# The expert stage of a decoder block, with TensorE's work written out in a fixed order that is one expert pair out of step

## The chip, the cores and the metric

The kernel runs on one core of one Trainium2 chip. The metric is device time in microseconds (us) for one launch. TensorE (PE in the rows) does the matmuls and the transposes, VectorE (DVE) and ScalarE (ACT) take results out of PSUM, GpSimd (POOL) gathers rows through an indirect DMA, and SyncE (SP) issues the plain loads and stores.

## The reference, cut to what matters

A block of 512 tokens with 1024 features goes through a token mixer, then through a mixture of 32 experts, of which each token uses two, then through a normalisation. The change is in the experts alone:

```
def hierarchical_moe(h, w_rg, b_rg, w_re, b_re, w1, w3, w2):
    t = h.reshape(B * S, D)                      # 512 x 1024
    ...                                          # group top-1, expert top-2 -> comb (512 x 32)
    for e in range(N_EXPERTS):                   # 32
        hid = jax.nn.silu(t @ w1[e]) * (t @ w3[e])          # 1024 x 512 each
        y = y + comb[:, e:e + 1] * (hid @ w2[e]).astype(jnp.float32)   # 512 x 1024
```

All weights are float32: w1, w3 and w2 of one expert are 2 MiB each, 192 MiB for the 32 experts.

## The kernel before

Experts are taken in 16 pairs (expert p and expert p + 16). A pair has 128 slots, 64 for each of its experts, and two pairs make a group, so there are 8 groups. For a group, `fetch` marks on VectorE which token sits in which slot (`sel0`), has TensorE turn that into row numbers and weights (`slot_weights`, bank `pw`), and gathers the tokens' rows into `xg` by two indirect DMAs. `experts` then does, for the group:

- rows: 16 transposes of `xg` in four blocks into the banks `gx`; ScalarE and VectorE each scale half of a block into `xt`.
- `slot_rows`: four transposes of `sel0` per pair (bank `pbk`), copied by ScalarE to `back`, which later puts the slots' results back on their tokens.
- `layer(q, "a")` and `layer(q, "b")`: the products of pair q with w1 (`ha`) and w3 (`hb`). Each is 16 float32 matmuls of 512 columns; they alternate between the two experts of the pair, which lie in the two halves of the array's columns (`tile_position`). The profile shows each such matmul as two instructions, so a product has 32 rows.
- `turned(q)`: four transposes (bank `pht`) of the gated hidden layer, copied by ScalarE to `ht`.
- `outputs(q, ht)`: the second layer, again 32 rows, into two banks `po`; VectorE weighs them (`high`) and splits them into two parts (`ohl`), with a ScalarE copy in between.
- `combine`: eight joins per group, four matmuls each (bank `pc`), which VectorE adds to `hx`. Before, the joins of a group are put in a list, `pending`, and are written out in the next group's `turned(0)`.

The weights come in loads of 1 MiB, issued by SyncE in a fixed order, into a ring of 16 such places (18 the first time round). A load waits until the load that had its place before has been used. 13 loads are issued ahead of the expert stage; `weights(p)` issues the rest as the program goes along. Before, the order of loads is pair by pair: w1, w3, w2. The last two pairs have a special order and w2 in narrower parts (`TAIL`).

What orders the engines: SyncE is always in the order of the code. For TensorE, VectorE and ScalarE a scheduler places the instructions of the groups, by its own estimate of times, and only the end of the last group (`ORDER`) is written out by hand.

Of the kernel before, what the change touches and what calls it, by code (L numbers as in the profile page):

```python
# [8 lines left out]
F32 = mybir.dt.float32  # L9
# [16 lines left out]
H = 4  # L26
# [34 lines left out]
def kernel(ctx: ExitStack, tc: tile.TileContext, a, dbg=None):  # L61
# [17 lines left out]
    def after(ins, other):  # L79
        tc.add_manual_dep(raw_ins(ins), raw_ins(other).name, NOSYNC, reason="order")  # L80
# [659 lines left out]
    def big(tag, name, shape, dt=F32):  # L740
        return pr.tile(list(shape), dt, tag=tag, bufs=SLOTS[tag], name=name)
# [451 lines left out]
    def count_passes(last):  # L1193
        pcn = bank("g", "pcn")
        for t in range(NT):
            after(T.matmul(pcn[:, 0:NE], onesb, ohs[:, t, :], start=(t == 0), stop=(t == NT - 1)), last)
# [16 lines left out]
    WORK = {"back": 3, "wsl": 4, "h": 1}  # L1213
# [12 lines left out]

    pending = []
# [58 lines left out]
    def fetch(n, cols, name):  # L1286

        xg = cp.tile([P, 2, D], F32, tag="U", bufs=2, name="xg" + name)
        wcol = {}
        for q in range(n):  # L1290
            for t in range(NT):
                V.tensor_scalar(sel0[:, t, q * P:(q + 1) * P], slotno, cols(q)[0][:, t], None, op0=ALU.is_equal)
            wcol[q], at = slot_weights(q, cols(q), name, True)
            G.indirect_dma_start(xg[:, q], None, rowsd, bass.IndirectOffsetOnAxis(at.bitcast(U32), 0), bounds_check=S - 1, oob_is_err=False)
        return xg, wcol

    def experts(n, cols, wts, name, ready=None, following=None, early=False, tail=False, alone=False):


        NSL = n * P  # L1300
        sel2 = sel0
        if alone:
            ready = fetch(n, cols, name)
        xt = big("rows", "xt" + name, [P, ND, 2 * P])
        for kk in range(ND // 2):
            if early:
                o = gathered[kk]
            else:
                o = bank("bg" if kk % 2 == 0 else "tr", f"gx{name}{kk}")
                for k2 in range(2):  # L1310
                    for q in range(n):
                        c = k2 * 256 + q * P
                        T.transpose(o[:, c:c + P], ready[0][:, q, (2 * kk + k2) * P:(2 * kk + k2 + 1) * P], ident)
            for k2 in range(2):
                k = 2 * kk + k2
                os = o[:, k2 * 256:k2 * 256 + NSL]
                if k2 == 0:
                    last = A.activation(xt[:, k, 0:NSL], os, AF.Identity, bias=b2x[:, k:k + 1], scale=a2x[:, k:k + 1])
                else:
                    V.tensor_scalar(xt[:, k, 0:NSL], os, a2x[:, k:k + 1], b2x[:, k:k + 1], op0=ALU.mult, op1=ALU.add)  # L1320
        if early:
            for t in range(NT):
                token_weights(t, last)
        wcol = {} if early else ready[1]
        back, res = [], []

        def slot_rows(q, last_h=None):
            pt = bank("tr", f"pbk{name}{q}")
            for t in range(NT):
                tr = T.transpose(pt[:, t * P:(t + 1) * P], sel2[:, t, q * P:(q + 1) * P].bitcast(F32), ident)  # L1330
                if early:
                    after(tr, last_h)
# [6 lines left out]
        if not early:  # L1339
            slot_rows(0)  # L1340
        s1s, lasts = {}, {}
        halves = [slice(0, 2), slice(2, 4)] if tail else [slice(0, 4)]

        def layer(q, m):
# [3 lines left out]
            for k in range(ND):  # L1348
                for e in range(2):
                    ins = T.matmul(o[64 * e:64 * e + 64, :], xt[:, k, q * P + 64 * e:q * P + 64 * e + 64], w[wn, e, k // 4][:, k % 4, :],  # L1350
                                   start=(k == 0), stop=(k == ND - 1), tile_position=(0, 64 * e))
                    if early and q == 0 and m == "b" and k + e == 0:
                        after(ins, lasts["a"])
            lasts[m] = ins
# [8 lines left out]
        def turned(q):  # L1363

            if early and q == 0:
                for i in range(n):
                    slot_rows(i, lasts["b"])
                count_passes(lasts["b"])

            while pending:  # L1370
                pending.pop(0)()
            if q == 0 and n > 1 and not early:
                slot_rows(1)
# [3 lines left out]
            ht = wk("back" if tail and q == 0 else "h", f"ht{name}{q}", [P, 4, P])  # L1377
            for h in halves:
                A.copy(ht[:, h], pt.rearrange("p (f s) -> p f s", f=4)[:, h])  # L1379
            return ht  # L1380

        def hidden(q):
            layer(q, "a")
            layer(q, "b")
            return turned(q)

        def outputs(q, ht):

            w, ws = wts(q), wcol[q]
# [19 lines left out]

        def combine(qs, c0, c1, t):  # L1410
# [8 lines left out]
        if not tail:  # L1419
            pieces = [(0, 512), (512, D)]  # L1420
            for q in range(n):
                if q == n - 1 and following is not None:
                    following()
                steps = outputs(q, hidden(q))
                for c, p in enumerate(pieces):
                    for f in steps:
                        f(c, *p)
            joins = [lambda p=p, t=t: combine(range(n), *p, t) for p in pieces for t in range(NT)]
            if alone:
                for f in joins:  # L1430
                    f()
            else:
                pending.extend(joins)
            return
        m = [outputs(0, hidden(0))]
        norm, add, root, write = final(f"f{name}", layer(1, "a"))

        def second():
            layer(1, "b")
            m.append(outputs(1, turned(1)))  # L1440

        sums = {"A": (0, 512), "B": (512, 768), "C": (768, D)}

        def join(x, t):
            combine([1], *sums[x], t)
            norm(t, "ABC".index(x), *sums[x], V if (x, t) in (('A', 3), ('C', 1), ('C', 3)) else G)

        STEPS = {"M": lambda q, c: m[q][0](c, *TAIL[q][c]), "H": lambda q, c: m[q][1](c, *TAIL[q][c]), "L": lambda q, c: m[q][2](c, *TAIL[q][c]),
                 "X": second, "J": lambda c, t: combine([0], 512 * c, 512 * c + 512, t), "S": lambda t: add(t), "R": lambda t: root(t, 2), "W": lambda t: write(t, (640, 640, 640, 640)[t])}
        STEPS.update({x: lambda t, x=x: join(x, t) for x in sums})  # L1450
        ORDER = """M00 H00 L00 M01 H01 L01 M02 H02 J00 J01 L02 J02 J03 M03 H03 L03 J10 J11 J12 J13 X
                   M10 H10 L10 M11 H11 L11 M12 H12 M13 L12 H13 A0 A1 L13 M14 H14 A2 A3 L14 M15 H15
                   B0 B1 L15 B2 B3 S1 C0 R0 C1 R1 W0 C2 R2 W1 C3 R3 W2 W3"""
        with tc.manual_schedule(engines={mybir.EngineType.PE, mybir.EngineType.DVE, mybir.EngineType.Activation}):
            for step in ORDER.split():
                STEPS[step[0]](*map(int, step[1:]))

    fetched = {}
    pair_columns = lambda g: (lambda q: (sp[:, :, 2 * g + q:2 * g + q + 1], wp[:, :, 2 * g + q]))
    for g in range(NP // 2):  # L1460
        more_pairs = g + 1 < NP // 2
        experts(2, pair_columns(g), lambda q: weights(2 * g + q), f"g{g}_", fetched.get(g),
                (lambda: fetched.__setitem__(g + 1, fetch(2, pair_columns(g + 1), f"g{g + 1}_"))) if more_pairs else None, g == 0, not more_pairs)
# [3 lines left out]
    with tc.For_i(0, more):  # L1467
        V.tensor_scalar(base, base, float(CAP), None, op0=ALU.add)
        slots("m")
        with tc.For_i(0, NP) as p:  # L1470
# [7 lines left out]
            experts(1, lambda q: (spc, wpc[:, :, 0]), lambda q: got, "m_", alone=True)  # L1478
# [29 lines left out]
```

## Time and profile before

| what | value |
|---|---|
| median of 3 runs | 1057.96 us (1057.88 to 1058.51) |
| the profiled execution, its device time | 1057.19 us |
| the profiled execution, its span | 1055.5 us |
| mean granted TensorE clock over the span | 0.979 |
| TensorE busy | 982.8 us, 93% |
| VectorE, ScalarE, GpSimd busy | 55%, 32%, 18% |
| DMA | 283.96 MB, mean 269 GB/s |

The rows come from the profiled execution, so sums are made against its span of 1055.5 us; its device time is 1.7 us more, and the median of the three runs is 0.8 us above that. The expert stage begins at 531 us. A busy TensorE is not one at its peak: a matmul counts as busy from its start to its modelled end, also when its other half of the columns stands empty.

### The profile page before, as it was taken

To read this page: it belongs to the slowest core of one execution; us is meant where nothing else is said; L and a number is where in the kernel's file an instruction comes from. 1 tells how busy PE (TensorE), PEld (TensorE's weight loads), DVE (VectorE), ACT (ScalarE), POOL (GpSimd) and SP (SyncE) were. 2 spreads that over 40 slices of the span, in tenths; PEclk is the share of its full clock that TensorE was granted. 3 is DMA by queue.
4 is the path that set the end of the run, shared out by engine and by line. 5 is a ranking of instruction groups with operands and counts; after the bars stand their busy time and mean duration, and the time that the engine had idled before them with its cause. 6 is when DMAs were issued, how large, how long until landed. Compare 5 with 4: busy or idle time off the path is not lost. (4 is left out here: it accounts for less than half of the span.)

```text
span 1055.5 us, 13713 instructions
## 1 busy us (share of the span) xinstructions
PE 982.8 (93%) x5250; PEld 628.2 (60%) x5250; DVE 576.3 (55%) x1057; ACT 336.7 (32%) x685; POOL 188.8 (18%) x122
## 2 busy tenths in 40 slices
PE   7899999889898999899999999999999999999993
PEld 3678899888776888787743534443444434434342
DVE  7978998997898875953632314131141312313136
ACT  6556333346355444434931101010110101101024
POOL 4514334124322122210310000000000000000005
PEclk9999999989998999999999999999999999999997
DMA  9943233226766573589199999999999989899912
GB/s 281 239 132 81 80 96 86 61 60 191 248 222 217 149 231 99 181 305 377 61 403 421 421 421 421 420 421 418 421 409 409 422 341 414 350 408 397 332 31 82
DMA packets 122409, 283.96 MB, mean 269 GB/s; under 512 B 10819, under 2 KB 87339, under 8 KB 99044
## 3 DMA queue, kind: packets, MB, share of 16 engines
q1 hardware_dynamic: 112700, 252.21, 64.0%
q10 hardware_dynamic: 7624, 27.27, 7.6%
q0 software_dynamic: 2016, 3.56, 0.9%
q8 instruction: 43, 0.70, 0.3%
q14 instruction: 26, 0.21, 0.1%
HBM read 282.61 MB, written 4.19 MB: 272 GB/s over the span
## 5 line engine op out<-in xcount | busy, mean ns | idle before, releaser
L383 POOL TENSOR_TENSOR low<-raww,hiw 128x1024 fp32r<-128x1024 f32 x36 | 91.6, 2544 | 213.2 <-ACT hiw L409 199.6
L1398 PE MATMUL pog<-p_w,htg 128*64 128x512 f32 x448 | 121.1, 599 | 7.0 <-ACT htg L1379 7.0
L392 PE MATMUL fmw<-uhi,low 128*128 128x512 f32 x224 | 91.3, 408 | 0.0
L392 PE MATMUL fmw<-ulo,hiw 128*128 128x512 f32 x224 | 90.5, 404 | 0.0
L69 DVE SCALAR_TENSOR_TENSOR conv<-z,cols,conv 128x511 f32<-128x511 f32 (+14 forms) x120 | 88.6, 738 | 3.5
L392 PE MATMUL fmw<-uhi,hiw 128*128 128x512 f32 x224 | 89.8, 401 | 0.0
L1398 PEld LDWEIGHTS pog<-p_w,htg 128*64 128x64 f32 x448 | 38.5, 136 | 69.8 <-issue 59.1
L66 DVE TENSOR_TENSOR s1g<-s1g,hbg 128x512 f32<-128x512 f32 (+1 forms) x18 | 11.1, 627 | 124.9 <-PE hbg L1350 114.3
L1415 PE MATMUL pcg<-ohlg,backg 128*128 128x512 f32 (+1 forms) x264 | 71.7, 407 | 5.4 <-DVE hx L66 2.4
L69 DVE SCALAR_TENSOR_TENSOR pog<-pog,wslg,ga2r 128x512 f32<-128x512 f32 (+2 forms) x38 | 25.6, 674 | 93.1 <-PE pog L1398 92.2
L66 DVE TENSOR_TENSOR hx<-hx,pcg 128x512 f32<-128x512 f32 (+1 forms) x76 | 49.0, 655 | 46.9 <-PE pcg L1415 46.6
L392 PE MATMUL tm<-hiw,ulo 128*128 128x256 f32 x256 | 74.0, 290 | 0.0
L392 PE MATMUL tm<-low,uhi 128*128 128x256 f32 x256 | 73.8, 289 | 0.0
L392 PE MATMUL tm<-hiw,uhi 128*128 128x256 f32 x256 | 73.6, 289 | 0.0
L409 ACT CAST hiw<-raww 128x1024 fp32r<-128x1024 f32 x44 | 46.0, 1047 | 81.6 <-issue 43.4
L1415 PEld LDWEIGHTS pcg<-ohlg,backg 128*128 128x128 f32 x264 | 46.6, 190 | 37.2 <-issue 9.0
L1403 ACT CAST ohlg<-pog 128x512 fp32r<-128x512 f32 (+2 forms) x38 | 19.6, 517 | 109.9 <-DVE pog L69 95.4
L392 PEld LDWEIGHTS tm<-hiw,uhi 128*128 128x128 f32 x256 | 49.7, 195 | 0.8 <-issue 0.5
L392 PEld LDWEIGHTS tm<-low,uhi 128*128 128x128 f32 x256 | 49.7, 194 | 0.7 <-issue 0.2
L392 PEld LDWEIGHTS tm<-hiw,ulo 128*128 128x128 f32 x256 | 49.8, 194 | 0.5 <-issue 0.2
L1379 ACT COPY htg<-phtg 128x512 f32<-128x512 f32 (+1 forms) x18 | 9.5, 538 | 124.0 <-PE phtg L1376 115.8
L392 PEld LDWEIGHTS fmw<-uhi,low 128*128 128x128 f32 x224 | 42.7, 190 | 9.7
(454 smaller groups left out, 1923.7 us busy)
## 6 DMA issues: line engine op xcount, KB each, us to landing
p_w<-in_w SPq DMA_DIRECT2D x182, 1024.0 KB, 14.9
raww<-in_w_in SPq DMA_DIRECT2D x44, 512.0 KB, 4.0
adaw<-in_w_ada SPq DMA_DIRECT2D x32, 256.0 KB, 5.7
aw_ga<-in_w_ada ACTq DMA_DIRECT2D x8, 1024.0 KB
p_w2part<-in_w SPq DMA_DIRECT2D x12, 512.0 KB, 10.4
aw_a<-in_w_ada ACTq DMA_DIRECT2D x4, 1024.0 KB
aw_b<-in_w_ada ACTq DMA_DIRECT2D x4, 1024.0 KB, 7.3
aw_bf<-in_w_ada_f ACTq DMA_DIRECT2D x4, 1024.0 KB, 5.9
```

The costliest lines, as they stand in the source:

```text
L66: return V.tensor_tensor(out, in0, in1, op=op)
L69: return V.scalar_tensor_tensor(out, in0, scalar, in1, op0=op0, op1=op1)
L383: (V if turn[0] % LO_EVERY < lo_v[0] else G).tensor_tensor(lo, raw, hi.bitcast(F32), op=ALU.subtract)
L392: ins = T.matmul(*args, **kw)
L409: copy = A.copy(hi, raw)
L1379: A.copy(ht[:, h], pt.rearrange("p (f s) -> p f s", f=4)[:, h])
L1398: T.matmul(o[64 * e:64 * e + 64, :], ht[:, f, 64 * e:64 * e + 64], w["w2", e, c][:, f, :] if tail else w["w2", e, f // 2][:, f % 2, c0:c1] ...
L1403: A.copy(ohl[:, 0, c0:c1], prods[c])
L1415: T.matmul(o, back[z][:, t * P:(t + 1) * P], res[z][:, i, c0:c1], start=(z == qs[0] and i == 0), stop=(z == qs[-1] and i == 1))
```

## The change

TensorE's order in the expert stage is now written out by hand for all groups, and one pair is put between a pair's products and its second layer: w1 of a pair, then the transposes of the pair before, then w3, then the second layer of the pair before. The loads follow that order of use: w1 and w3 of pair p, then w2 of pair p - 1. `back` moves into the unused half of the tile that `xg` has, so that the buffers of the hidden layer can be three. VectorE and ScalarE are still placed by the scheduler.

```diff
-    order2 = [(0, 0, 8), (1, 0, 4), (0, 8, 12), (1, 4, 13)]
-    todo = [step for steps in todo[:-2] for step in steps] + [step for i, b, e in order2 for step in todo[NP - 2 + i][b:e]]
+    order2 = [(1, 0, 4), (0, 8, 12), (1, 4, 13)]
+
+    use = list(todo[0][0:8])
+    for p in range(1, NP - 1):
+        use += todo[p][0:8] + todo[p - 1][8:12]
+    todo = use + [step for i, b, e in order2 for step in todo[NP - 2 + i][b:e]]
...
-        while todo and count[0] < 12 * p + len(order):
+        while todo and count[0] < 12 * p + 8 + len(order):
...
-    WORK = {"back": 3, "wsl": 4, "h": 1}
+    WORK = {"back": 1, "wsl": 4, "h": 3}
...
-        xg = cp.tile([P, 2, D], F32, tag="U", bufs=2, name="xg" + name)
+        both = cp.tile([P, 4, D], F32, tag="U", bufs=2, name="xg" + name)
+        xg, room = both[:, 0:2], both[:, 2:4]
...
-            b = wk("back", f"back{name}{q}", [P, S], F32R)
+            b = rooms[0][:, 0, q * S:(q + 1) * S].bitcast(F32R)
...
+    with tc.manual_schedule(engines={mybir.EngineType.PE}):
+        for g, x in enumerate(X):
+            before = X[g - 1] if g else None
+            x["rows"](fetched)
+            if g:
+                x["slot_rows"](0)
+                x["slot_rows"](1)
+            x["layer"](0, "a")
+            if g:
+                before["turned"](1)
+            x["layer"](0, "b")
+            if g:
+                before["second"](1)
             else:
-                pending.extend(joins)
...
+                x["slot_rows"](0)
+                x["slot_rows"](1)
+                count_passes()
+            if g < NGR - 1:
+                fetched = fetch(2, pair_columns(g + 1), f"g{g + 1}_")
+            silu = x["layer"](1, "a")
+            x["turned"](0)
+            if g:
+                before["joins"]()
+            if g < NGR - 1:
+                x["layer"](1, "b")
+                x["second"](0)
+            else:
+                x["ending"](silu)
```

`second(q)` is the second layer of a pair, `joins()` the eight joins of a group, and `ending` the tail of the last group, in the same hand-written `ORDER` as before.

Where a group begins, this is what stood on TensorE before (the pair that ends is `pog_1`, the group that begins has `hag_0` and `xtg__6875`; the eight joins are `pcg`):

```order
L1398 MATMUL pog_10_6851<-p_w_6790,htg_1_6848 64x512
L1398 MATMUL pog_11_6863<-p_w_6790,htg_1_6848 64x512
L1330 MATMUL pbkg_1_7020<-ident,sel_4372 128x128 x4
L1398 MATMUL pog_10_6851<-p_w_6792,htg_1_6848 64x512
...
L1415 MATMUL pcg_000_6972<-ohlg_1_6850,backg_1_6717 128x512
L1350 MATMUL hag_0_6935<-p_w_6794,xtg__6875 64x512
L1415 MATMUL pcg_000_6972<-ohlg_1_6850,backg_1_6717 128x512
L1415 MATMUL pcg_100_6978<-ohlg_0_6726,backg_0_6601 128x512 x2
...
L1415 MATMUL pcg_05120_6996<-ohlg_0_6726,backg_0_6601 128x512
L1350 MATMUL hag_0_6935<-p_w_6796,xtg__6875 64x512
L1350 MATMUL hag_0_6935<-p_w_6794,xtg__6875 64x512
```

The scheduler had cut the products into pieces of one, two or seven matmuls and put transposes and joins between them. In the changed kernel the same place, where a group begins, reads:

```order
L1380 MATMUL pog_01_6532<-p_w_6287,htg_0_6451 64x512
L1380 MATMUL pog_01_6532<-p_w_6289,htg_0_6451 64x512
L1318 MATMUL gxg_0_6545<-ident,xgg__6372 128x128 x4
L1318 MATMUL gxg_1_6552<-ident,xgg__6372 128x128 x4
L1318 MATMUL gxg_2_6559<-ident,xgg__6372 128x128 x4
L1318 MATMUL gxg_3_6566<-ident,xgg__6372 128x128 x4
L1337 MATMUL pbkg_0_6573<-ident,sel_4372 128x128 x4
L1337 MATMUL pbkg_1_6579<-ident,sel_4372 128x128 x4
L1350 MATMUL hag_0_6609<-p_w_6291,xtg__6544 64x512
L1350 MATMUL hag_0_6609<-p_w_6293,xtg__6544 64x512
...
L1364 MATMUL phtg_1_6628<-ident,s1g_1_6444 128x128 x4
```

Here the six blocks of transposes stand together, with no product among them, and the 16 matmuls of each product follow each other, the two experts in turn.

On VectorE in the changed kernel, at the same place, the weighing of the second layer (`pog`), its split (`ohlg`) and the scaling of the rows (`xtg`) stand in this order:

```order
L69 SCALAR_TENSOR_TENSOR pog_01_6532<-pog_01_6532,wslg_0_6076,ga2r 128x512
L66 TENSOR_TENSOR ohlg_0_6519<-pog_01_6532,ohlg_0_6519 128x512
L1325 TENSOR_SCALAR xtg__6544<-gxg_0_6545,a2x,b2x 128x256
L1325 TENSOR_SCALAR xtg__6544<-gxg_1_6552,a2x,b2x 128x256
L1325 TENSOR_SCALAR xtg__6544<-gxg_2_6559,a2x,b2x 128x256
L1295 TENSOR_SCALAR sel_4372<-slotno,sp 128x128 x4
L1325 TENSOR_SCALAR xtg__6544<-gxg_3_6566,a2x,b2x 128x256
```

In the kernel before, the scaling of a group's rows stood ahead of the weighing of the pair that ended:

```order
L1320 TENSOR_SCALAR xtg__6567<-gxg_2_6582,a2x,b2x 128x256
L1292 TENSOR_SCALAR sel_4372<-slotno,sp 128x128 x4
L69 SCALAR_TENSOR_TENSOR pog_10_6543<-pog_10_6543,wslg_1_6160,ga2r 128x512
L69 SCALAR_TENSOR_TENSOR pog_11_6555<-pog_11_6555,wslg_1_6160,ga2r 128x512
L66 TENSOR_TENSOR ohlg_1_6542<-pog_10_6543,ohlg_1_6542 128x512
```

So the rows' scaling moved behind the last weighing and split of the pair before.

## Rows read from the trace of the kernel before

**Rows 1.** Windows: stretch, its length, busy us by engine, TensorE clock, DMA share, GB/s.
```profile
540.00:560.00 20.00, 20.00 (x112) 8.67 (x110) 4.85 (x21) 1.76 (x3) 2.21 (x2) 1.00 1.02 421
...
760.00:780.00 20.00, 18.98 (x82) 8.81 (x79) 9.01 (x20) 3.68 (x7) 0.00 (x0) 1.00 1.01 420
780.00:800.00 20.00, 18.44 (x83) 7.73 (x83) 3.88 (x9) 1.74 (x3) 1.98 (x2) 1.00 0.99 394
...
900.00:920.00 20.00, 19.99 (x76) 8.70 (x72) 8.30 (x13) 1.76 (x3) 0.00 (x0) 1.00 0.86 345
```

**Rows 2.** Timeline, TensorE (start, length): second transposes of the third and seventh groups.
```profile
688.81 0.66 PE L1376 MATMUL phtg<-ident,s1g 128*128 128x128 f32 x4 [0.84 <-DVE s1g L66]
...
953.10 0.66 PE L1376 MATMUL phtg<-ident,s1g 128*128 128x128 f32 x4 [0.58 <-DVE s1g L66]
```

**Rows 3.** Timeline of TensorE, a product cut into pieces.
```profile
903.45 1.07 PE L1350 MATMUL hag<-p_w,xtg__6875 128*64 128x512 f32 x2
...
908.00 3.65 PE L1350 MATMUL hag<-p_w,xtg__6875 128*64 128x512 f32 x14
```

**Rows 4.** Waits of TensorE from 530 us: us in total, times, longest.
```profile
PE phtg L1376 <- DVE s1g L66: 9.8, 14, 0.9
PE pog L1398 <- ACT htg L1379: 7.5, 12, 0.7
```

**Rows 5.** Timeline of TensorE, products and joins that stand in one piece.
```profile
594.87 3.06 PE L1415 MATMUL pcg<-ohlg,backg 128*128 128x512 f32 x12
597.77 0.60 PE L1330 MATMUL pbkg<-ident,sel 128*128 128x128 f32 x4
...
938.30 7.09 PE L1350 MATMUL hag<-p_w,xtg__6875 128*64 128x512 f32 x32
945.17 7.09 PE L1350 MATMUL hbg<-p_w,xtg__6875 128*64 128x512 f32 x32
```

**Rows 6.** Timeline, the rows of the fourth group and who takes them out.
```profile
696.23 1.53 PE L1313 MATMUL gxg<-ident,xgg__5827 128*128 128x128 f32 x12
697.14 1.48 ACT L1318 ACTIVATE xtg__5951<-gxg,b2x,a2x 128x256 f32<-128x256 f32 x3 [7.05 <-PE gxg L1313]
697.74 1.46 DVE L1320 TENSOR_SCALAR xtg__5951<-gxg,a2x,b2x 128x256 f32<-128x256 f32 x3 [8.98 <-ACT xtg__5951 L1318]
```

**Rows 7.** Timeline around the end of a second layer, which TensorE left at 938.30.
```profile
937.66 1.66 DVE L69 SCALAR_TENSOR_TENSOR pog<-pog,wslg,ga2r 128x512 f32<-128x512 f32 x2 [7.67 <-PE pog L1398]
...
939.23 1.44 DVE L66 TENSOR_TENSOR ohlg<-pog,ohlg 128x512 fp32r<-128x512 f32 x2
939.36 0.59 ACT L1403 CAST ohlg<-pog 128x512 fp32r<-128x512 f32 x1 [0.31 <-DVE pog L69]
```

**Rows 8.** Timeline of TensorE, the start of the expert stage.
```profile
531.32 7.86 PE L1350 MATMUL hag<-p_w,xtg__4999 128*64 128x512 f32 x32
539.01 7.03 PE L1350 MATMUL hbg<-p_w,xtg__4999 128*64 128x512 f32 x32
545.98 0.66 PE L1330 MATMUL pbkg<-ident,sel 128*128 128x128 f32 x4
```

**Rows 9.** Timeline of TensorE, the tail: second layer of pair 14, w3 of pair 15.
```profile
1001.63 0.59 PE L1398 MATMUL pog<-p_w2part,htg 128*64 128x256 f32 x2
...
1017.14 7.09 PE L1350 MATMUL hbg<-p_w,xtg__7183 128*64 128x512 f32 x32
```

**Rows 10.** Timeline of the SyncE queue: the first loads issued once the stage has begun.
```profile
527.62 12.39 SPq L945 DMA_DIRECT2D p_w<-in_w  x9
```

**Rows 11.** DMA queues from 480 us, the gathers' queue: packets, MB, share.
```profile
q0 software_dynamic: 2016, 3.56, 1.7%
```

**Rows 12.** A window in which the narrow parts of w2 are loaded.
```profile
990.00:1000.00 10.00, 8.70 (x48) 3.43 (x44) 0.75 (x2) 0.65 (x2) 0.00 (x0) 1.00 1.08 348
```

**Rows 13.** Windows around the one fall of the clock in this stage.
```profile
526.00:527.00 1.00, 0.25 (x3) 0.10 (x1) 0.75 (x3) 1.00 (x2) 0.24 (x1) 1.00 0.00 0
...
530.00:531.00 1.00, 1.00 (x7) 1.00 (x6) 0.16 (x1) 0.75 (x2) 0.00 (x0) 0.50 0.85 287
```

More of the change, by code (lines that the diff above doesn't have):

```diff
@@ L1306, in experts @@
             if early:
-                o = gathered[kk]
-            else:
[L1309 to L1327, printed above, removed]
+                for t in range(NT):
+                    token_weights(t, last)
+                rooms.append(cp.tile([P, 4, D], F32, tag="U", bufs=2, name="room" + name)[:, 2:4])
+            else:
+                wcol.update(ready[1])
+                rooms.append(ready[2])
+        def slot_rows(q):
@@ L1349, in layer @@
                 for e in range(2):
[L1350 to L1354, printed above, removed]
+                    T.matmul(o[64 * e:64 * e + 64, :], xts[0][:, k, q * P + 64 * e:q * P + 64 * e + 64], w[wn, e, k // 4][:, k % 4, :],
+                             start=(k == 0), stop=(k == ND - 1), tile_position=(0, 64 * e))
             ov = o.rearrange("p (i f) -> p f i", f=4)
@@ L1376, in turned, with outputs @@
                 T.transpose(pt[:, f * P:(f + 1) * P], s1s[q][:, f], ident)
-            ht = wk("back" if tail and q == 0 else "h", f"ht{name}{q}", [P, 4, P])
+            ht = hts[q] = wk("back" if tail and q == 0 else "h", f"ht{name}{q}", [P, 4, P])
             for h in halves:
                 A.copy(ht[:, h], pt.rearrange("p (f s) -> p f s", f=4)[:, h])
[L1380 to L1389, printed above, removed]
+        def outputs(q):
+            w, ws, ht = wts(q), wcol[q], hts[q]
             ohl = big("wo1", f"ohl{name}{q}", [P, 2, D], F32R)
@@ L1408, in outputs, with second @@
             return products, high, low
+        pieces = [(0, 512), (512, D)]
+        def second(q):
+            steps = outputs(q)
+            for c, p in enumerate(pieces):
+                for f in steps:
+                    f(c, *p)
         def combine(qs, c0, c1, t):
@@ L1435, in experts @@
[L1435 to L1463, printed above, removed]
+        def joins():
+            for p in pieces:
+                for t in range(NT):
+                    combine(range(n), *p, t)
@@ new lines, in experts @@
+        return dict(rows=rows, slot_rows=slot_rows, layer=layer, turned=turned, second=second, joins=joins, ending=ending)
+    pair_columns = lambda g: (lambda q: (sp[:, :, 2 * g + q:2 * g + q + 1], wp[:, :, 2 * g + q]))
+    NGR = NP // 2
+    X = [experts(2, pair_columns(g), lambda q, g=g: weights(2 * g + q), f"g{g}_", g == 0, g == NGR - 1) for g in range(NGR)]
+    fetched = None
+    with tc.manual_schedule(engines={mybir.EngineType.PE}):
[11 more added lines that the diff above has]
+                before["second"](1)
+            else:
+                x["slot_rows"](0)
[10 more added lines that the diff above has]
+                x["second"](0)
+            else:
+                x["ending"](silu)
@@ L1477 @@
                 step()
-            experts(1, lambda q: (spc, wpc[:, :, 0]), lambda q: got, "m_", alone=True)
+            x = experts(1, lambda q: (spc, wpc[:, :, 0]), lambda q: got, "m_")
+            x["rows"](fetch(1, lambda q: (spc, wpc[:, :, 0]), "m_"))
+            x["slot_rows"](0)
+            x["layer"](0, "a")
+            x["layer"](0, "b")
+            x["turned"](0)
+            x["second"](0)
+            x["joins"]()
         norm, add, root, write = final("r_")
```

84 lines of the change are left out of this document (45 added, 39 removed).

## The prediction, made before the run

> **What bounds the kernel now.** I read the windows of the expert stage first, because the change touches nothing else. From 531 us to the end it takes half of the span. In its first half the DMA engines are busy all the time and move about 420 GB/s; later their share falls to 0.86 in places, while TensorE's busy time is between 18.4 and 20.0 of 20 us in these rows [rows 1]. So both are near full, and the question is which waits for which. The period of a group decides it: from the third to the seventh group the same transposes come 264.3 us apart, 66.1 us per group [rows 2]. The loads of a group are 24 MiB, 25.2 MB, and a gather of 0.5 MB (3.56 MB in seven groups [rows 11]): 25.7 MB, at 421 GB/s 61.0 us. TensorE is the slower of the two by 5 us per group; the loads, which began 13 MiB ahead, run into places that are still in use.
>
> Then I read TensorE's timeline for what it does in 66.1 us. Its waits that the trace names are small: 9.8 us for the gating before the transposes and 7.5 us for the copy behind them over the whole stage [rows 4], some 2.3 us per group, because these stand in a chain (w3, gate, transposes, copy, second layer) with nothing between. The larger loss is in the products themselves. A product in one piece occupies 6.87 us for its 16 matmuls (938.30 to 945.17 [rows 5]), 0.43 us each, since two of them run side by side in the two halves of the columns. One matmul alone takes 1.07 us, and seven take 3.65 us, 0.52 each [rows 3]: a matmul that has lost its partner pays for both halves. Of six products in a group about three are cut in this way.
>
> **The group after, step by step.** Six products, each in one piece: 6.87 us and 6.97 us (539.01 to 545.98 [rows 8]), I take 6.92: 41.5 us. Eight joins of four matmuls: twelve occupy 2.90 us (594.87 to 597.77 [rows 5]), so 32 occupy 7.7 us. Ten blocks of four small matmuls or transposes (four of rows, two of slots, two of hidden layers, two of weights): three take 1.53 us [rows 6], so 5.1 us. Together 54.3 us.
>
> The waits that go: the transposes and the copy now have a product of 6.9 us between them and what they need, and between them and who needs them; gate and copy are far shorter, so I set both waits to 0. If that cover were gone, the 2.3 us would be back.
>
> The waits that come stand at the head of a group. Four blocks of rows use one bank of the kind `bg` and two of the kind `tr`, in turn, and the third block needs the bank of the first. Ahead of the rows VectorE has, in its new order, the last weighing and the last split of the pair that ended. These last until 1.0 us and 2.4 us after TensorE has left the second layer, with ScalarE's copy until 1.65 us between them (939.32, 940.67 and 939.95 against 938.30 [rows 7, 5]). Clearing a block is then 0.5 us of each engine [rows 6]. So the first block is clear at 2.9 us and not at 2.0 (698.23 against 696.23), the third block starts at 3.0, the first slot block follows at 4.0, the third is clear at 5.0, and the fourth, behind two or four marks of slots on VectorE, at about 6. The last slot block, which takes a `tr` bank again, ends at about 6.5. The pure work is 3.1 us (six blocks), so 3.4 us are waited. Bounds: 3.1 us for the whole head, if nothing waits, and 10 us, if each of the four blocks takes the 2.0 us of a lone clearing behind the 2.4 us of the split. I take 6.5, because its parts have rows. Behind the waiting blocks stand all products of the group on TensorE, and with them the places that the loads wait for. The gather itself was issued one product, eight joins and two more products earlier, some 29 us, and is not late. For the two weight blocks of `fetch` I add 0.5 us of wait (the bank is free only behind the weighing, 1.0 us); bounds 0 and 1.5.
>
> A group: 54.3 + 3.4 + 0.5 = 58.2 us.
>
> **The sum for TensorE.** The first two products are unchanged and end at 545.98 [rows 8]. Then come slots, count and fetch together, six blocks, 3.0 us, and 1.8 us of waits for VectorE's eight marks (0 to 4): 550.8. Three products and a block of transposes: 572.1. Six groups of 58.2: 921.3. The last group: head 6.5, four products 27.7, two blocks 1.0, joins 7.7, the rows of the final normalisation 2.7 (four blocks, 0.7 of waits for ScalarE's copies), and the second layer of pair 14 with its joins. That took 15.5 us before (1001.63 to 1017.14 [rows 9]), with two of those row blocks and a stray matmul in it, so 14.1. That makes 59.7, and w3 of pair 15 starts at 981.0. From there the order is the old one: 1055.5 - 1017.14 = 38.4. End: 1019.4 us.
>
> The new place of w2 in the loads' order costs nothing here, since loads and uses are in one order on both queues. At the start it could: w2 of pair 0 is no longer among the 13 loads that are there. It is the fourth to seventh load from 527.62, in place at 545, and wanted at 565. `back` in the other half of the gathered tile is the same copy of ScalarE, and nothing else touches that half.
>
> **The sum for the loads.** 13 of 192 MiB are there before. 179 MiB, 187.7 MB, and 3.56 MB of gathers are 191.3 MB, at 421 GB/s 454.3 us; from 527.62 [rows 10] to 981.9. The 8 MiB of narrow parts go at about 348 GB/s [rows 12], 4.2 us more: 986.1. But w1 of pair 15 is the load that counts: behind it lie 4 MiB of narrow w2 (12.05 us), w3 (10.0) and again narrow w2 (12.05), so it is complete at 952.0. Half a product (3.5), transposes, joins, normalisation rows and the second layer (25.0) follow, so w3 starts at 980.5, and the end is 1018.9 us.
>
> Both chains end at 1019. They meet at every load, and the later sets the pace at each place; a stretch such as 780 to 800 at 394 GB/s [rows 1] costs 1.3 us of loads alone. I take 3 us for this, between 0 and 10. Span 1022.3; 1.7 us around it and 0.8 us to the median make 1025 us, 3.1% less than 1057.96.
>
> The Trainium skill speaks against this: "DMA: Bandwidth & Descriptors", in its Specifications, gives a core some 358 GB/s from HBM. By that figure the loads alone would last 534 us, an estimate, and the kernel would end near 1100; the trace disagrees, with 420 GB/s and more in the rows from 540 to 780 [rows 1].
>
> **Rivals.** A difference of 0.2%, 2 us, is about what a measurement of this kernel can tell from no change.
>
> *Longer heads of groups.* Each us more in the head costs 7 us, as seven groups have one. At 10 us the end is 24.5 us later, 1049. There is a second way to it: before the stage, TensorE was busy for only a quarter of a us in 526 to 527, and the clock then fell to 0.50, 1.2 of 2.4 GHz, around 530 to 531 [rows 13]; the first product took 7.86 us where the next took 7.03 [rows 8]. The new heads are idle for more than half of their time. At 2.3 us for each (0.8 in the product, 1.5 in the transposes) that is 16 us, 1041. For it: the single bank and VectorE's order. Against: waits of 0.9 us have not brought the clock down in this stage.
>
> *Slower or equal: the loads do not keep 421 GB/s.* The end lies 33 us behind the last load. For an end at 1055.5 it would have to come at 1022.4, the 191.3 MB in 491 us: 390 GB/s. The rate in 780 to 800 was 394 with a share of 0.99, so such stretches exist; against it, the twelve stretches of 20 us from 540 to 780, of which the first and the last have rows, were at 418 to 422. From 390 downwards the gain is gone, and at 380 the kernel takes about 1071.
>
> *Equal: the losses only change their name.* TensorE in a fixed order can no longer step over a wait. If heads and fetch together waited 9.1 us instead of 3.9, the group would last 63 us and the end would be the old one. Nothing in the rows reaches that.
>
> *Faster: the heads are hidden.* If VectorE clears the rows as fast as the transposes come, TensorE ends up to 24 us earlier, but the loads still end at 1018.9, so the time is about 1021; only narrow parts at the full rate would bring it to 1016 or below.
>
> That the change does nothing can be left out: the order shows the products in one piece.
>
> **Chances.** Forecast, 1016 to 1036: 0.60. Longer heads, 1036 to 1053: 0.22. Loads at 390 GB/s or less: 0.05. Losses renamed: 0.05. Below 1016: 0.08. Faster 0.90 (the first two and the last), same 0.03, slower 0.07. The range leaves out the two slower rivals, some of the longer heads and some of what lies below: 1014 to 1046.
>
> **What would show it.** Right: products of 6.9 us in one piece throughout; a period of 58 to 61 us per group; no waits of the transposes on the gate; a wait of the third block of rows on VectorE of about 2 us; w3 of pair 15 starting near 983; the DMA share at 1.0 until 985. Wrong: a period over 62; a clock below 1.00 at the heads of groups; waits of the products on loads of more than some 10 us in total; a rate of the loads under 410 GB/s while their share is 1.0.

## The result, and the profile after

| | device time, us | ratio to before, 95% interval |
|---|---|---|
| before, 4 runs beside it | 1057.92 (1056.78 to 1058.51) | |
| the changed kernel, 4 runs | 1029.65 (1028.08 to 1031.11) | 0.9734 (0.972 to 0.9748) |

The change makes the kernel 28.3 us faster, 2.7%. The forecast was 1025. The profiled execution took 1028.08 us, its span is 1026.4, and w3 of pair 15, the last product but one, starts 5 us later than forecast.

The timeline of TensorE in the changed kernel, its first product and then one group and its neighbours (start, length), answers to [rows 2, 3, 5]:

```profile
532.12 7.09 PE L1350 MATMUL hag<-p_w,xtg__5001 128*64 128x512 f32 x32 [0.28 <-ACT xtg__5001 L1323]
...
585.12 7.09 PE L1350 MATMUL hbg<-p_w,xtg__5320 128*64 128x512 f32 x32
592.04 7.04 PE L1380 MATMUL pog<-p_w,htg 128*64 128x512 f32 x32
...
600.13 7.09 PE L1350 MATMUL hag<-p_w,xtg__5320 128*64 128x512 f32 x32
...
607.57 7.71 PE L1405 MATMUL pcg<-ohlg,roomg__5094 128*128 128x512 f32 x32
615.21 7.09 PE L1350 MATMUL hbg<-p_w,xtg__5320 128*64 128x512 f32 x32
...
629.10 1.09 PE L1318 MATMUL gxg<-ident,xgg__5454 128*128 128x128 f32 x8
631.85 1.09 PE L1318 MATMUL gxg<-ident,xgg__5454 128*128 128x128 f32 x8 [1.66 <-DVE xtg__5626 L1325]
...
686.25 1.09 PE L1318 MATMUL gxg<-ident,xgg__5760 128*128 128x128 f32 x8
```

Every product of these groups stands in one piece of 6.9 to 7.0 us from start to start, the joins take 7.64, and a group takes 57.15 us (629.10 to 686.25), where it took 66.1.

Later the same timeline looks different. These are the last two heads of groups, the second half of w1 of pair 15, and w3 of pair 15 (answers to [rows 9]):

```profile
863.85 1.09 PE L1318 MATMUL gxg<-ident,xgg__6678 128*128 128x128 f32 x8
...
926.28 1.09 PE L1318 MATMUL gxg<-ident,xgg__6984 128*128 128x128 f32 x8
...
961.34 3.65 PE L1350 MATMUL hag<-p_w,xtg__7158 128*64 128x512 f32 x14 [1.23 <-DMA p_w<-in_w]
...
988.14 7.09 PE L1350 MATMUL hbg<-p_w,xtg__7158 128*64 128x512 f32 x32
```

The last period is 62.4 us. The waits of TensorE from 530 us on (us in total, times, longest) say for what:

```profile
PE pog L1380 <- DMA p_w<-in_w: 5.8, 6, 1.4
...
PE hag L1350 <- DMA p_w<-in_w: 1.2, 1, 1.2
```

Gate and copy, 17 us before [rows 4], are gone from the list but for 1 us in the tail; loads have come in. The windows (columns as in [rows 1]) show the queues that feed them:

```profile
760.00:780.00 20.00, 19.96 (x94) 8.91 (x90) 3.94 (x9) 1.17 (x2) 0.00 (x0) 1.00 1.02 422
...
920.00:940.00 20.00, 17.55 (x90) 7.46 (x88) 4.81 (x8) 5.08 (x10) 0.00 (x0) 1.00 1.01 421
```

The DMA engines are busy all the time at 421 GB/s, up to 940, and TensorE is not. From some 820 us on the loads are the bound, and no longer TensorE.

### The profile page after: what moved, and what is told of

Same layout as the page of the kernel before. It is cut to its first block, busy times and chain, and to the rows that moved or that the text cites. A ratio compares the mean times of both kernels' runs of the same rounds, so it can differ in the third digit from the quotient of the medians.

```text
span 1026.4 us, 13698 instructions
## 1 busy us (share of the span) xinstructions
PE 952.5 (93%) x5250; PEld 619.6 (60%) x5250; DVE 582.2 (57%) x1057; ACT 337.2 (33%) x685; POOL 188.3 (18%) x122
## 3 DMA queue, kind: packets, MB, share of 16 engines
q0 software_dynamic: 2016, 3.56, 0.9%
## 5 line engine op out<-in xcount | busy, mean ns | idle before, releaser
L1380 PE MATMUL pog<-p_w,htg 128*64 128x512 f32 x448 | 105.6, 594 | 5.8 <-DMA p_w<-in_w 5.8
L1380 PEld LDWEIGHTS pog<-p_w,htg 128*64 128x64 f32 x448 | 34.6, 137 | 74.5 <-issue 60.6
L392 PEld LDWEIGHTS fmw<-ulo,hiw 128*128 128x128 f32 x224 | 42.9, 192 | 9.9
L392 PEld LDWEIGHTS fmw<-uhi,hiw 128*128 128x128 f32 x224 | 42.8, 191 | 9.8
L1356 ACT ACTIVATE s1g<-hag 128x512 f32<-128x512 f32 x16 | 9.6, 598 | 104.5 <-PE hag L1350 104.5
## 6 DMA issues: line engine op xcount, KB each, us to landing
p_w<-in_w SPq DMA_DIRECT2D x182, 1024.0 KB, 19.8
```

Source lines behind the costliest of these rows:

```text
L392: ins = T.matmul(*args, **kw)
L1356: return A.activation(s1s[q], ov, AF.Silu)
L1380: T.matmul(o[64 * e:64 * e + 64, :], ht[:, f, 64 * e:64 * e + 64], w["w2", e, c][:, f, :] if tail else w["w2", e, f // 2][:, f % 2, c0:c1] ...
```

## The experiments

Theory A: what the change gains is that products are no longer cut; TensorE would now need some 57 us per group, and the loads (61 us per group, begun at 528.85) bind the end. Rivals: TensorE's order and heads of groups still bind (B); the gain is the skew, which covers gate and copy, not the unbroken products (C); the new order of the loads does it, or matters not at all (D). Times are medians in us; each ratio is to the kernel before on the same chip. Runs without an interval are single ones.

| run | time | ratio (95%) |
|---|---|---|
| cut product | 1058.9 | |
| cut between pairs | 1031.75 | |
| no skew | 1031.04 | 0.9752 (0.9719 to 0.9784) |
| pair loads | 1055.73 | |
| fewer bytes | 1013.97 | |
| stores on ScalarE | 1029.12 | 0.973 (0.9708 to 0.9752) |
| four loads early | 1031.41 | 0.9743 (0.9727 to 0.976) |
| three before the third store | 1022.6 | 0.9668 (0.965 to 0.9685) |
| w3 before w2 | 1028.65 | 0.9713 (0.9689 to 0.9739) |
| four early, and w3 | 1030.25 | 0.9731 (0.9715 to 0.9748) |
| three early, and w3 | 1021.57 | 0.9646 (0.9623 to 0.9669) |
| no skew, three early | 1030.7 | 0.9742 (0.9726 to 0.9759) |

**What a cut costs.** One product of a group is cut by the joins that stood behind it.

```diff
-            silu = x["layer"](1, "a")
+            silu = x["layer"](1, "a", before["each_join"]() if g else ())
...
+                    if between:
+                        between.pop(0)()
```

> The changed kernel with one product in each group cut: the eight joins stand one by one behind the first eight matmuls of w1 of the group's second pair, so that these eight have no partner; the same instructions otherwise. Theory A (a matmul that lost its partner pays for both halves): 8 x 0.43 to 8 x 0.64 = 3.4 to 5.1 us per group, a period of 60 to 62 us in the groups that TensorE binds, and 1037 to 1046 us. Rival C (cutting is free, the losses before were the waits in the chain): 1028 to 1031 us, periods as in the changed kernel.

The timeline of TensorE there: the product's matmuls 1 and 2, the join between them, and the start of w3, which follows the product, the other joins and a block of transposes.

```profile
664.18 1.04 PE L1351 MATMUL hag<-p_w,xtg__5626 128*64 128x512 f32 x2
665.15 1.19 PE L1408 MATMUL pcg<-ohlg,xgg__5196 128*128 128x512 f32 x4
666.27 1.07 PE L1351 MATMUL hag<-p_w,xtg__5626 128*64 128x512 f32 x2
...
685.38 4.94 PE L1351 MATMUL hbg<-p_w,xtg__5626 128*64 128x512 f32 x22
```

Eight cuts bring some 6.5 us per group (periods of 62.6 to 63.8 where 57.15 stood), and the whole gain of the change is lost: 1058.9. Rival C falls, but both figures lie above theory A's (60 to 62, 1037 to 1046). A cut has two prices, the partner and the change of the array's division. The next run has the same number of cuts, always behind two matmuls:

```diff
-                    if between:
+                    if between and e:
```

> As the run with the cut product, but the eight joins stand behind every second matmul of the same product, so that two matmuls that lie in the two halves of the columns always follow each other: as many cuts, but no matmul without a partner. Theory A (what a cut costs is the partner that is lost): eight pairs of 1.07 us at most for 6.95, and joins of 1.13 for 0.95, 1.5 to 3.2 us per group and not 6.5; groups of 58.5 to 60.5 us, 1029 to 1036 us. Rival G (each change between product and join costs, whatever stands next to it): periods of 63.5 us, 1055 to 1060 us.

The same place in the timeline of TensorE:

```profile
660.07 1.08 PE L1351 MATMUL hag<-p_w,xtg__5626 128*64 128x512 f32 x4
661.08 1.20 PE L1408 MATMUL pcg<-ohlg,xgg__5196 128*128 128x512 f32 x4
662.21 1.08 PE L1351 MATMUL hag<-p_w,xtg__5626 128*64 128x512 f32 x4
...
677.62 7.09 PE L1351 MATMUL hbg<-p_w,xtg__5626 128*64 128x512 f32 x32
```

Two matmuls take 1.08 us and one takes 1.07: the partner costs nothing, and one without it pays for both. From the product's start to the start of w3 it is 17.55 us here (660.07 to 677.62), 21.20 with the cut product (664.18 to 685.38) and 15.08 uncut (600.13 to 615.21 in the changed kernel). This run has 14 changes between product and full-width matmuls more than the uncut kernel: 2.47 us, 0.18 each, which had no place in the prediction. The cut product has two changes more again and eight lost partners: 3.65 us, less 0.35 for the two, so 0.41 for a partner, close to theory A's 0.43. A new product alone costs nothing that shows (w3 with the second layer behind it lasts 6.92 us, 585.12 to 592.04). Rival G falls: 1031.75 and not 1055, with periods of 58.9 to 60.1 us. The Trainium skill, "TensorEngine Tiling (Array Packing)", Key Properties, says that a change of the tiling mode drains TensorE and that different tiles can run at once. Both agree with these two timelines, which add the prices; that the 0.18 us is this drain is not shown by itself.

**The skew alone.** Each pair is finished before the next begins; products stay whole, loads pair by pair as before.

```diff
...
             x["layer"](0, "a")
-            if g:
-                before["turned"](1)
             x["layer"](0, "b")
             if g:
-                before["second"](1)
+                before["joins"]()
...
+            x["turned"](0)
             if g < NGR - 1:
+                x["second"](0)
                 fetched = fetch(2, pair_columns(g + 1), f"g{g + 1}_")
             silu = x["layer"](1, "a")
-            x["turned"](0)
-            if g:
-                before["joins"]()
             if g < NGR - 1:
                 x["layer"](1, "b")
-                x["second"](0)
+                x["turned"](1)
+                x["second"](1)
...
```

> TensorE's order is still written by hand with every product in one piece, but each pair is finished before the next begins (w1, w3, transposes, second layer), and the loads are again pair by pair; the joins of a group stand between w3 and the transposes of the next group's first pair. Theory A (unbroken products give the gain, and the loads bind at the end): the gate and the two copies are waited for again, 2 to 2.5 us per group, so a group takes 59 to 60 us, still less than its loads; 1028 to 1034 us. Rival C (the skew gives the gain by covering gate and copy): the gain shrinks by 7 x 2.3 = 16 us or more, 1044 to 1058 us.

Waits of TensorE from 530 us on:

```profile
PE pog L1376 <- ACT htg L1363: 10.0, 15, 0.7
PE phtg L1360 <- DVE s1g L66: 6.6, 8, 0.9
```

The waits for copy and gate are back, 16.6 us, and the time is 1031.04; its interval and that of the change lie over each other. Rival C falls as stated: nearly all of the gain is there without the skew. No matmul waits for a load in this kernel (its loads of weights into the array wait 2.7 us in all), so it is TensorE that binds here, at 59 to 60 us per group, and 1.4 us above the skewed order that the loads bind. That the two come out so close is a coincidence of two bounds; the last run below separates them.

**The order of the loads alone.** The skewed order of TensorE with the old order of loads.

```diff
...
-    use = list(todo[0][0:8])
-    for p in range(1, NP - 1):
-        use += todo[p][0:8] + todo[p - 1][8:12]
-    todo = use + ...
...
+    todo = [step for steps in todo[:-2] for step in steps] + ...
...
```

> The changed kernel with the old order of the loads (w1, w3, w2 pair by pair), TensorE's skewed order kept. Theory A: w2 of a pair now holds its places over the next pair's w1 and w3, and the load of the w1 after that can start only when w2 has been used, some 1.7 us before the second layer ends; two loads take 5 us and 2 us until they land. So TensorE stands some 5 us before a product in each pair, in every other pair partly under the head of a group: 62 to 66 us per group, 1040 to 1065 us. Rival D (the order of the loads does not matter, 16 places are enough): 1028 to 1031 us.

The waits of TensorE from 530 us on in that kernel:

```profile
PE hag L1346 <- DMA p_w<-in_w: 14.5, 12, 2.2
PE hbg L1346 <- DMA p_w<-in_w: 3.8, 3, 1.3
```

w1 and w3 wait for their loads, the first period is 56.4 us and the others alternate between 61 and 68 (67.6, 61.2, 67.5, 60.9, 68.7), and 1055.73 is the time of the kernel before within 0.4%. Rival D falls: with 16 places the loads must come in the order in which TensorE uses them, and the skewed order is worth something only with its own order of loads. That order of loads under an unskewed TensorE was not run.

**Who binds the end.** Fewer bytes, the same instructions.

```diff
+        if not tail:
+            todo = [(key, src) for key, src in todo if key[0] != "w3" or key[2] == 0]
...
+                    half = w[wn, e, k // 4] if (wn, e, k // 4) in w else w["w1", e, 1]
```

> Left out: in the first 14 pairs the second half of w3 is not loaded, and the product takes the second half of w1 in its place (the result is another). TensorE's instructions and their order are the same, the loads of a group are 51 us and not 61. Theory A (loads bind the end): the time of TensorE alone comes out: periods of 56.5 to 57.5 us in every group, the last head near 914, w3 of pair 15 near 971, no wait for a load after 800, 1010 to 1014 us. Rival B (heads and order bind): no change, 1026 to 1031 us.

TensorE's timeline, the first product, the first and last heads of groups and w3 of pair 15:

```profile
534.41 7.21 PE L1353 MATMUL hag<-p_w,xtg__5001 128*64 128x512 f32 x32
...
575.00 1.09 PE L1320 MATMUL gxg<-ident,xgg__5196 128*128 128x128 f32 x8
...
916.39 1.09 PE L1320 MATMUL gxg<-ident,xgg__6936 128*128 128x128 f32 x8
...
973.56 7.09 PE L1353 MATMUL hbg<-p_w,xtg__7108 128*64 128x512 f32 x32
```

Six groups take 341.4 us, 56.9 each, to the last, and TensorE waits for no load. 1013.97: theory A, not B. From the first product (534.41 here, 532.12 in the changed kernel) to w3 of pair 15, TensorE needs 439.2 us; with all bytes it takes 456.0. So the loads cost 16.9 us.

**Loads that begin earlier.** If the loads bind, an earlier start should show at the end. They stand in SyncE's queue behind four stores of the rows, the last at 528.75. First, all four stores move to ScalarE's queue:

```diff
-        SY.dma_start(rowsd[us], scaled[:, t % 2].rearrange("p k i -> p (k i)"))
+        A.dma_start(rowsd[us], scaled[:, t % 2].rearrange("p k i -> p (k i)"))
```

> The stores of the rows (rowsd) go out from ScalarE's queue, so that SyncE's loads do not stand behind them; all else is the changed kernel. Theory A (from group 5 on the loads bind, and they started at 528.85): the first loads go when their places come free, near 520, 8 to 9 us earlier; after five of them the next wait for the places of the first products (532 to 536), so some 4 to 6 us stay. TensorE's waits for loads after 820 shrink by that, w1 of pair 15 is complete near 956, and the time is 1023 to 1026 us. Rival B (TensorE's heads and order bind): 1028 to 1031, no change. In both the first five groups keep their periods of 56 to 58 us.

Then the stores are back on SyncE, with four loads ahead of the last one:

```diff
+        if t == NT - 1:
+            for _ in range(4):
+                todo.pop(0)()
         SY.dma_start(rowsd[us], scaled[:, t % 2].rearrange("p k i -> p (k i)"))
```

> All four stores of the rows go out from SyncE again, but four loads (those into the places of w_out, free from 516 to 520) are issued ahead of the last store; the others stay behind it at 528.8. Four MiB take 10 us, so they have landed by 530 and the last store is not held up as it was when all loads went first. Theory A (the loads bind from group 5 on, and what counts is when they start): 10 us of loads are gained, some 4 of them lost again while the next loads wait for the places of the first products (531.5 to 535.7); the first head of a group stays at 572 to 573, TensorE's waits for loads after 800 shrink by 4 to 6 us, 1024 to 1026 us. Rival B (TensorE's order binds): 1028 to 1031 us.

Neither was faster (1029.12 and 1031.41, both above theory A's range), as rival B had it, although the run with fewer bytes says that the loads bind. ScalarE's waits between 520 and 545 us show why. In the changed kernel:

```profile
ACT xtg__5001 L1323 <- DMA rowsd<-scaled: 3.0, 1, 3.0
```

The same wait with the stores on ScalarE's queue:

```profile
ACT xtg__5001 L1323 <- DMA rowsd<-scaled: 6.7, 1, 6.7
```

And with four loads early:

```profile
ACT xtg__5009 L1326 <- DMA rowsd<-scaled: 11.3, 1, 11.3
```

The scaled rows of the first group (`xt`) are written where `scaled` was, so ScalarE waits until the last store has read it. With loads in front, that store of 0.5 MB is slow. TensorE's first product in the run with four early loads:

```profile
539.98 8.45 PE L1353 MATMUL hag<-p_w,xtg__5009 128*64 128x512 f32 x32 [7.18 <-ACT xtg__5009 L1326]
```

It starts at 539.98 and not at 532.12. The loads after the first 18 need the places of that product, so they stop too: from 540 to 548 the DMA share was 0.22. What the early loads gained was given back through a store. If so, three loads ahead of the third store should keep the gain:

```diff
-        if t == NT - 1:
-            for _ in range(4):
+        if t == NT - 2:
+            for _ in range(3):
```

> In both runs with early loads the last store of the rows stood behind loads, and ScalarE's first scaling of rows, which writes where that store reads, waited for it: 6.7 and 11.3 us, with the first product 4.8 and 7.9 us late. Here three loads are issued ahead of the third store (521.5), so 3 MiB (7.5 us) are through by 527 to 529, before the last store goes at 528.3. Theory A (loads bind the end, the early loads were given back through the store): the first product starts at 532 to 533, the first head stays near 573, the waits for loads after 800 shrink, 1023 to 1027 us. Rival F (early loads are worth nothing, whatever the store does): 1028 to 1031 us.

TensorE's timeline there: the first product, the second half of w1 of pair 15, and w3 of pair 15.

```profile
531.92 7.83 PE L1353 MATMUL hag<-p_w,xtg__5007 128*64 128x512 f32 x32
...
955.69 3.65 PE L1353 MATMUL hag<-p_w,xtg__7158 128*64 128x512 f32 x14 [1.24 <-DMA p_w<-in_w]
...
982.49 7.09 PE L1353 MATMUL hbg<-p_w,xtg__7158 128*64 128x512 f32 x32
```

And ScalarE's wait for the store:

```profile
ACT xtg__5007 L1326 <- DMA rowsd<-scaled: 3.0, 1, 3.0
```

It is what it was in the changed kernel, the first product is in time, w1 of pair 15 comes 5.65 us earlier (955.69 against 961.34), and w3 of pair 15 too. 1022.6 us, 0.9668: the interval lies below that of the changed kernel, and the time 0.4 us below the forecast. Theory A holds, and rival F falls.

**The tail.** w3 of pair 15 goes ahead of the second layer of pair 14, by itself and with either form of early loads.

```diff
-    order2 = [(1, 0, 4), (0, 8, 12), (1, 4, 13)]
+    order2 = [(1, 0, 7), (0, 8, 12), (1, 7, 13)]
...
-            ORDER = """M00 H00 L00 M01 ...
+            ORDER = """Y M00 H00 L00 M01 ...
```

Here `Y` is the product of w3 of pair 15, which `X` did before.

> Only the end: the loads of w3 of pair 15 come before the narrow w2 of pair 14, and TensorE does w3 of pair 15 ahead of the second layer of pair 14. If the end is bound by TensorE's work behind the arrival of w1 of pair 15 (theory A), only the waits for the last gate and copy go, 1 to 2 us, and the parts of w2 of pair 14 arrive 983 to 984, 1 to 2 us late: 1027 to 1030 us. Rival E (the last load bounds the end): the last load comes at the same time, near 992, but finds less work behind it (7 us of w3): 1021 to 1025 us.

> Four loads early and w3 of pair 15 ahead of the second layer of pair 14, together. Theory A: the sum of the two, 1022 to 1026 us. Rival B: 1027 to 1031 us.

> The three early loads, and w3 of pair 15 ahead of the second layer of pair 14, together. Theory A: 1 us below the run with three early loads alone, 1022 to 1026 us. Rival F: 1027 to 1030 us.

Each is about 1 us below its partner without the edit (1028.65 to 1029.65, 1030.25 to 1031.41, 1021.57 to 1022.6). No pair of intervals is apart, so the single gain is not shown; the sign is three times the same. Rival E, 1021 to 1025 for the edit alone, falls: behind w1 of pair 15 lies TensorE's own work. The run with four early loads missed its forecast of 1022 to 1026 for the reason found above; the one with three came out 0.4 us below its own. Three loads early and w3 first is the fastest kernel here: 1021.57, 0.9646.

**Skew and loads together.** The order without the skew gets the three early loads of the run above.

> The order without the skew, with three loads ahead of the third store. That order showed no wait of TensorE for a load and a steady 60.0 us per group, so TensorE binds it. Theory H (without the skew TensorE binds, with it the loads): early loads give nothing here, 1029 to 1032 us, and the skew is worth some 7 to 9 us once the loads come earlier. Rival I (the loads bind both orders, and the skew is worth 1 us): 1022 to 1025 us.

1030.7, no change against 1031.04: without the skew TensorE binds, and loads that come earlier are of no use. With the skew the same edit takes the ratio from 0.9734 to 0.9668. So the skew is worth nothing that can be measured with the loads as the change has them, and 0.7%, 8 us, once they begin earlier (0.9742 against 0.9668, intervals apart). That is not all of it: with the three early loads the loads still bind the skewed order, whose w3 of pair 15 starts 450.6 us after the first product (531.92 to 982.49), where TensorE alone needs 439.2.

## Why the prediction was right, and where it was off

**What bounded before, and the mechanism.** Right. TensorE was the bound, and the cut products were its main loss: the order without skew, where products are whole and gate and copy are waited for, has nearly all of the gain, and one product cut again takes it back. TensorE's groups of instructions (count, busy us, mean ns, idle time before them) show it directly, first for the group from 819.36 to 885.77 in the kernel before, then for the one from 629.10 to 686.25 in the changed kernel:

```profile
L1398 PE MATMUL pog<-p_w,htg 128*64 128x512 f32 x64 | 18.3, 601 | 1.2 <-ACT htg L1379 1.2
L1350 PE MATMUL hag<-p_w,xtg__6567 128*64 128x512 f32 x64 | 16.5, 597 | 0.0
L1350 PE MATMUL hbg<-p_w,xtg__6567 128*64 128x512 f32 x64 | 15.4, 595 | 0.0
L1415 PE MATMUL pcg<-ohlg,backg 128*128 128x512 f32 x32 | 8.8, 411 | 0.0
...
L1380 PE MATMUL pog<-p_w,htg 128*64 128x512 f32 x66 | 14.7, 592 | 0.0
L1350 PE MATMUL hag<-p_w,xtg__5626 128*64 128x512 f32 x64 | 14.2, 595 | 0.1
L1350 PE MATMUL hbg<-p_w,xtg__5626 128*64 128x512 f32 x64 | 14.2, 595 | 0.0
```

Products are busy for 50.2 us there and 43.1 here, joins for 8.8 and 7.7: 8.2 us, of the 9.3 by which the group became shorter; gate and copy add 2.7, and longer waits at the head take some back. The price of a matmul without a partner was right (1.07 us for one or for two); that each change of the array's division costs 0.18 us more was missing. So was a second way to lose a partner, two matmuls of one expert in a row, as in the first two lines of the order before:

```profile
897.00 1.93 PE L1398 MATMUL pog<-p_w,htg 128*64 128x512 f32 x4
```

They take 1.93 us, where two that lie in the two halves take 1.08.

**The group of 58.2 us.** 57.15 in the changed kernel and 56.9 without the bound of loads. Products (41.8 us against 41.5) and joins (7.64 against 7.7) were right to 0.3 us. Mis-sized were the head, 5.6 to 6.1 us (4.9 in the first) where 6.5 was taken, in which the third block waits 1.66 us for VectorE, and the two weight blocks, 1.1 us where 1.5 was counted. The 2.3 us of gate and copy went, as forecast.

**The sum for TensorE.** w3 of pair 15 was to start 449.7 us after the first product (531.3 to 981.0); TensorE alone needs 439.2. Of the 10.5 us too much, six groups of 58.2 for 56.9 are 7.8, the last group 2.5 (57.2 for 59.7).

**The sum for the loads.** Here the prediction failed in size. w1 of pair 15 was to be complete at 952.0, and came at 961.3. The windows of the changed kernel give the parts:

```profile
528.85:540.00 11.15, 9.92 (x53) 4.58 (x55) 5.65 (x40) 6.87 (x19) 0.89 (x1) 1.00 0.98 384
540.00:940.00 400.00, 378.05 (x1804) 166.70 (x1802) 108.10 (x232) 53.83 (x98) 14.08 (x14) 1.00 1.01 421
940.00:961.34 21.34, 18.21 (x82) 5.75 (x79) 3.65 (x6) 1.45 (x3) 0.00 (x0) 1.00 0.96 386
528.85:961.34 432.49, 406.18 (x1933) 177.02 (x1934) 117.40 (x278) 62.14 (x119) 14.98 (x15) 1.00 1.01 418
```

The first load went at 528.85, 1.2 us later than before. The rate was 421 for 400 us but 384 and 386 at the two ends, where I had it at 421 throughout: 3.1 us (432.5 us at 418 move what 429.4 move at 421). And 180.8 MB had been moved by then, though the loads up to this one and the gathers are 178.7 MB (167 MiB and 3.56 MB): 2.1 MB, 5 us. The queues of that window say what it was: 0.3 MB went through the two queues of instructions, 0.5 MB is the last store of the rows, issued at 528.75, and neither had a place in the sum. The other 1.3 MB, 3 us, must be of loads that stand behind w1 of pair 15: the sum took loads to finish strictly one behind the other, but a load takes 19.8 us from issue to landing (median) and 2.5 us of the rate, so some eight are in flight. These shares were worked out and not tried by themselves. From w1 to the start of w3 it was 26.8 us (961.34 to 988.14) where 28.5 was taken.

**Both meet: 3 us.** This term fell. It was to be what the two chains cost each other, with both taken to end at 1019. They were not equally long: TensorE alone would have reached w3 of pair 15 at 971.3 (532.12 and 439.2), the loads let it at 988.1, 16.9 us later. And from 540 to 940 us the loads ran at 421 GB/s, so TensorE held them up nowhere there: the chain of the loads by itself gives the end. That the total came out 4.65 us off (1029.65 for 1025) is luck in part. The loads' sum was 7.5 us too short (1018.9 for a span of 1026.4), the 3 us for a meeting made up for some of it, and TensorE's sum, 10 us too long, came out beside it by chance.

**The tail of 38.4 us.** 38.3 (988.14 to 1026.4). The start of w2 cost nothing, as forecast: the second layer of pair 0 follows w3 without a gap.

**The rivals.** Longer heads: no, and the clock stayed up, as a window of the changed kernel at a head shows:

```profile
686.00:692.00 6.00, 3.13 (x24) 2.42 (x23) 4.06 (x10) 3.01 (x6) 0.00 (x0) 1.00 1.02 425
```

TensorE is busy for half of it, and 1.00 is granted. Loads at 390 GB/s: no, 421 for 400 us. The 358 GB/s that the Trainium skill's "DMA: Bandwidth & Descriptors", Specifications, gives a core lie below what this core did. Losses renamed: no. Heads hidden: no; with the loads at 421 GB/s from 540 to 940 us it should have changed little, which was not tried.

**The list of signs.** Products of 6.9 us, no waits on the gate, the third block's wait and the DMA share (but for 0.96 from 940 to 961) were as named. The period of 58 to 61 was 56.5 to 58.5 in the first four groups, then 61.5 and 62.4, which is over the limit that I had named as wrong. The products' named waits for loads were 7 us, below the limit of 10, but the list does not hold all that they cost: the second layer from 884.41 to 895.67 took 11.3 us for 7. I read this as matmuls that run alone while the partner's weights are on their way; it was not measured by itself.

## What to carry to other kernels

Where matmuls run side by side in the halves of the columns, keep each product whole: in a trace, divide a product's time by its matmuls, and look for pieces with an odd count, or with two matmuls of the same half in a row. When a change shortens the bound, work out the next one from its first start to its last byte, not from its rate alone, and test it by taking its load away (here fewer bytes), which prices it in one run. Before an early transfer is pulled forward, look for a small one behind it on which a buffer's reuse waits.

## What the runs showed of the hardware

A matmul of 128x64 weights and 512 columns takes 1.07 us alone and 1.08 us with its partner; going to a full-width matmul or back costs about 0.18 us.

A store of 0.5 MB with four loads of 1 MiB ahead of it in SyncE's queue kept ScalarE waiting 11.3 us, from ScalarE's own queue beside loads 6.7 us, and 3.0 us with no load ahead of it and the first one issued 0.1 us behind it.

The clock did not fall in the heads of the changed kernel, but with the old order of loads it fell at some of TensorE's waits for a load (timeline of TensorE, then windows):

```profile
792.86 1.16 PE L1346 MATMUL hag<-p_w,xtg__6222 128*64 128x512 f32 x2 [1.02 <-DMA p_w<-in_w]
795.25 5.38 PE L1346 MATMUL hag<-p_w,xtg__6222 128*64 128x512 f32 x12 [1.23 <-DMA p_w<-in_w]
...
792.00:794.00 2.00, 1.14 (x2) 0.19 (x2) 0.79 (x3) 0.27 (x1) 0.00 (x0) 0.91 1.03 430
794.00:796.00 2.00, 0.77 (x3) 0.30 (x4) 0.00 (x0) 0.00 (x0) 0.00 (x0) 0.50 1.01 422
796.00:798.00 2.00, 2.00 (x8) 0.61 (x6) 0.00 (x0) 0.00 (x0) 0.00 (x0) 0.50 1.02 410
```

From 794 on it was 0.50, 1.2 of 2.4 GHz: TensorE had waited 1.02 us before the matmul at 792.86, waited 1.23 us more at the lower level, and stayed there while it was busy again. Such a wait does not always bring it down: in the changed kernel TensorE waited 1.42 us for a load before 827.41, and 1.00 was granted throughout. In that kernel's expert stage it fell once while there was work, to 0.61 on average from 550 to 554, after the small blocks for slots and count; the product there took 8.7 us (549.45 to 558.16).
